# A longer lag between a head's q and k loads and its scores, and the younger of two heads stepped first, in the attention of a streaming Conformer layer

## The chip, the cores and the metric

The kernel runs on one core of a Trainium2 chip. The metric is the device time of one execution in microseconds; the figure for the kernel before is the median of three runs. The profile is that of one further execution, and its own time is given beside its span below.

## The reference

One inference step of a one-layer streaming encoder, in float32, on a prompt of 2048 frames and a sample of 64 frames that has a cache of 256 keys and values. Cut to what matters:

```
h = rms_norm(x, g1) * (1 + sc1) + sh1
z = h @ w_in                         # GLU pair | q | k | v | two gates
u = glu_a * sigmoid(glu_b)           # -> causal depthwise conv, 31 taps
conv_out = silu(layer_norm(conv(u))) @ w_conv_out
q, k = rms_norm per head
s = (q @ k.T) / 8 + rel_bias[clip(q_pos - k_pos)]     # own chunk of 64 and the 8 before it
attn_out = (softmax(s) @ v) @ w_attn_out
x = x + gt1 * ((sig(g_conv) * conv_out + sig(g_attn) * attn_out) @ w_o)
x = x + gt2 * ((silu(gate) * up) @ w_ffn_out)         # gate, up from a normed x
```

There are 8 heads of 64. The outputs are both streams, the last 30 conv rows, and the last or new k and v rows.

## The kernel before, in words

**Two parts.** Part one makes everything up to the attention output and the conv output, which go to DRAM (`o_d`, `c_d`, `g_d`). Part two reads them back, merges them, and runs the output projection and the FFN. Every float32 product is made of three fp32r products of a high and a low part (`mm3`). Each Meter wrapper (L102 is its line, which is why nearly every instruction of the profile has that line) passes an instruction on and adds a planned duration to the load of its engine.

**Part one** runs over four blocks of 512 prompt frames (the first with the 64 sample frames beside them). `ORDER` gives the stages of a block: q projection, conv column group 0, k projection, group 1, v projection, groups 2 and 3, then 16 gate column groups. Through the whole of it TensorE's instructions run in the order in which the program writes them (`manual_schedule`, L1625); the order on the other engines, and that of the DMAs on SP's queue, is laid out by the framework.

**Lanes.** The matmuls of projections, conv groups and gates are the main line. Everything else is written as generators that sit in lanes: norms of the next block, q/k row work, attention (`attn`), conv norm, conv taps. After every 500 ns of planned TensorE time `Stream.tick` gives each lane a turn (`Lane.pump`, L141). A generator yields the planned TensorE time (`stream.load["pe"]`) from which it may be stepped again, or a condition. The lane takes the first of its `wide` oldest generators that is ready. For `attn` that is two wide, one step in 600 ns of plan at most, and none while the plan has VectorE over 3000 ns or ScalarE over 4000 ns ahead (`ATTN`). In block 3 the lane takes up to two steps a tick, without spacing. None of these times is a wait on the chip: they only fix where in TensorE's list a matmul stands. The waits on the chip are semaphores.

**Attention of a block.** After its v projection, `heads` (L1643) adds one generator per head: 8 prompt heads a block, and in block 0 also 8 heads of the sample (`"s"`), alternating with the prompt's; 40 in all, listed in `order`. `attend(i)` (L1495):

1. waits until head i - 1 is scored; `fetch(i)` (L1482) issues q, k (`load_qk`, L1418 and L1419: four DMAs on SP) and the bias band (`load_bias`, L1462: two more), unless the head before did it, and sets `loaded[i]`, the planned time from which scores may be given out.
2. yields `loaded[i]`, then for each of four tiles of 128 queries: four matmuls into `sc` (two PSUM banks, one buffer), VectorE's bias add with running maximum (`softmax_max`), ScalarE's exponential; between tiles it yields until VectorE is planned to be done.
3. after its last tile calls `fetch(i + 1)`. From block 1 on q2, kk and bias have one buffer each, so these loads can't start before the last scores are done.
4. scales, then, once head i - 1 is finished, five rounds of transposes (`ptp`), splits into `ph` and `pl` on ScalarE and VectorE, and products with v into `po`; at the end the output goes to `o_d`.

In block 0 the small q and k tiles of prompt head and sample head have separate places in the same buffers, so q and k of the next but one head are loaded early (`fetch_qk(i + 2)`).

At the end of part one `attn.drain()` (L1686) steps whatever is left, without regard to planned times. Part two's matmuls follow.

The lines that the change and the prediction touch:

```
DMA_LAG = 4000.0                                     # L50
attn = Lane(ATTN, ATTN_NS, wide=2)                   # L1608
entry = next((e for e in self.gens[: self.wide] if self.ready(e, stream)), None)
loaded[i] = stream.load["pe"] + DMA_LAG              # L1488
yield loaded[i]                                      # L1503
```

The planned duration of a matmul of n columns (n of 256 or more) is n / 2.4 ns. `DMA_LAG` also serves weights and other loads.

Of the kernel before, what the change touches and what calls it, by code (L numbers as in the profile page):

```python
# [39 lines left out]
ATTN = {"dve": 3000, "act": 4000}  # L40
ATTN_NS = 600.0
# [6 lines left out]
ON_ACT = (0, "s", 1, 2, 3)  # L48
ON_POOL = ()
DMA_LAG = 4000.0  # L50
OUT_LAG = 4000.0
CACHE_LAG = 16000.0
HEADS_NS = 2000.0
# [31 lines left out]
class Meter:  # L85


    def __init__(self, engine, name, stream):
        self.engine, self.name, self.stream = engine, name, stream
# [18 lines left out]
class Lane:  # L108

    def __init__(self, room, spacing=0.0, wide=1, burst=1):
        self.gens, self.room, self.spacing, self.wide, self.burst = [], room, spacing, wide, burst
        self.last = -1e9

# [25 lines left out]
    def pump(self, stream):  # L141
        for _ in range(self.burst):
            now = stream.load["pe"]
            if now - self.last < self.spacing or stream.full(self.room):
                return
            entry = next((e for e in self.gens[: self.wide] if self.ready(e, stream)), None)
            if entry is None:
                return
            self.last = now
            self.step(entry)  # L150
# [113 lines left out]
class Weights:  # L264
# [107 lines left out]
    def load(self, kind, sure=True):  # L372
# [8 lines left out]
        self.room[tag] -= 1  # L381
        self.landed[i] = self.stream.load["pe"] + DMA_LAG
        if self.items[i][0] == "fi":
# [178 lines left out]
def up_operands(f):  # L562

    ops = (["s2", "s3", "s1"] if f else ["s3", "s2", "s1"]) + ["a22"] + ["a12"] * (f >= EARLY) + ["a11"] * (EARLY <= f + 1 < NF) + ["s4"]
    return [(f + (op == "a11"), op) for op in ops]
# [50 lines left out]
def streaming_layer(ctx: ExitStack, tc: tile.TileContext, I, O):  # L618
    nc = tc.nc
    stream = Stream()  # L620
    pe, dve, act, gps = (
        Meter(e, n, stream) for e, n in ((nc.tensor, "pe"), (nc.vector, "dve"), (nc.scalar, "act"), (nc.gpsimd, "pool"))
    )
# [10 lines left out]
    def rows(prompt, sample, t, n):  # L634
        return prompt[t - SMP : t - SMP + n] if t >= SMP else sample[t : t + n]
# [824 lines left out]
    def load_bias(h):  # L1460
        for r in (0, HD):
            nc.sync.dma_start(  # L1462
                bias[r : r + HD, HD - r : 640 - r],
                bass.AP(tensor=rb_d.tensor, offset=rb_d.offset + 768 * h + HD, ap=[[1, HD], [1, 576]]),
            )
        return bias

    order, loaded, now = [], {}, {"scored": -1, "finished": -1, "bias": None}
# [8 lines left out]
    def fetch_qk(i):  # L1477
        if i < len(order) and ("qk", i) not in now:
            x, h = order[i]
            now["qk", i] = load_qk(x, h, *spans(x))  # L1480

    def fetch(i):  # L1482
        if i < len(order) and i not in loaded:
            x, h = order[i]
            fetch_qk(i)
            if now["bias"] is None or now["bias"][0] != h:
                now["bias"] = h, load_bias(h)
            loaded[i] = stream.load["pe"] + DMA_LAG  # L1488

    def fetch_v(i):  # L1490
        if i < len(order) and ("v", i) not in now:
# [3 lines left out]
    def attend(i):  # L1495
        x, h = order[i]
        q0, nq, k0, nk = spans(x)
        yield lambda: now["scored"] == i - 1
        fetch(i)
        fetch_v(i)  # L1500
        if not i:
# [4 lines left out]
        for t in range(0, nq, P):  # L1506
            n = min(P, nq - t)
            if x not in (0, "s"):
                ps = ps_a.tile([P, 2, 512], F32, tag="s", name="sc")
                for j in range(2):  # L1510
                    for d in range(2):
                        pe.matmul(ps[:, j, :320], q2[:, d, t : t + P], kk[:, t + 320 * j : t + 320 * j + 320], start=d == 0, stop=d == 1)
                w, src, bs = 640, ps[:, :, :320], bias[:, ::-1]
            else:
                w = nk if x == "s" else t + P

                if "banks" not in now:
                    sc = ps_a.tile([P, 2, 512], F32, tag="s", name="sc")
                    now["banks"] = [sc[:, 0:1], sc[:, 1:2]]
                ps = now["banks"].pop(0)  # L1520
                now["banks"].append(ps)
                for d in range(2):
                    pe.matmul(ps[:n, 0, :w], q2[:, d, t : t + n], kk[:, :w], start=d == 0, stop=d == 1)
                src, bs = ps[:n, 0:1, :w], bias[:n, 64:384][:, ::-1] if x == "s" else bias[:, :w][:, ::-1]
            pr, sm, free, ready = softmax_max(src, n, w, bs)
            tiles.append((pr, sm, n, w))
            if t + P < nq:
                yield free + PE_LAG, SCORE_ROOM
            else:
                fetch(i + 1)  # L1530
                if (x, order[min(i + 2, len(order) - 1)][0]) in ((0, 0), ("s", "s")):
                    fetch_qk(i + 2)
                now["scored"] = i
            if t:
                softmax_scale(*tiles[-2], x in ON_ACT)
# [69 lines left out]


    norm_lane, work = Lane({}, wide=NORM_W), Lane({}, wide=5)
    attn = Lane(ATTN, ATTN_NS, wide=2)  # L1608
    conv, tail = Lane({"dve": CONV_ROOM}, burst=4), Lane({})
    stream.lanes = [norm_lane, work, attn, tail, conv]  # L1610

# [268 lines left out]
    for s, (lo, hi) in enumerate(CBLOCKS):  # L1880
# [120 lines left out]
        class Operands:  # L2001


            def __init__(self, f0):
                self.ops = [(e, op) for f in (f0, f0 + 1) for e, op in up_operands(f)]
                self.at = 0
# [154 lines left out]
        def pieces():  # L2161
            return [(i, t, n, j) for i, (t, n) in enumerate(tiles) for j in range(2)]

        def scale():
# [4 lines left out]
            ends["gt"] = gt  # L2169
            yield stream.load["pe"] + DMA_LAG  # L2170
            for k, (i, t, n, j) in enumerate(pieces()):
# [21 lines left out]
        def load_ends():  # L2193
# [3 lines left out]
            for k, (i, t, n, j) in enumerate(pieces()):  # L2197
                nc.sync.dma_start(ends["x1"][k // 3][:n, k % 3], x1_d[t : t + n, 512 * j : 512 * j + 512])
            ends["landed"] = stream.load["pe"] + 2 * DMA_LAG

        def add_last(ws):

            for k, (i, t, n, j) in enumerate(pieces()):
# [14 lines left out]
                else:  # L2218
                    stream.at(stream.when("dve") + OUT_LAG, lambda out=out, dst=dst: nc.sync.dma_start(out, dst))
            for _ in ws:  # L2220
# [4 lines left out]
        def add_left(left):  # L2225

            for dst, x1, out in left:
                gps.tensor_tensor(dst, dst, x1, ALU.add)
                stream.at(stream.when("pool") + OUT_LAG, lambda out=out, dst=dst: nc.sync.dma_start(out, dst))
                yield stream.when("pool"), {"pool": 500}  # L2230

        def add_down(fs, ws):

            last = fs[-1] == NF - 1
            for i, (t, n) in enumerate(tiles):
# [15 lines left out]
                for j, ps in enumerate(pss):  # L2251
# [7 lines left out]
                    else:  # L2259
                        dve.tensor_tensor(ps, ps, dst, ALU.add)  # L2260
                        dst = dst[:n]
                        if t < SMP:
# [3 lines left out]
                        stream.at(  # L2266
                            stream.when("dve") + OUT_LAG,
                            lambda t=t, n=n, f=f, dst=dst: nc.sync.dma_start(rows(y_p, y_s, t, n)[:, f], dst),
# [89 lines left out]
```

## Time and profile before

| | us |
|---|---|
| median of three runs | 3014.24 (3009.83 to 3023.16) |
| profiled execution, its own time | 3015.03 |
| its span in the profile | 3013.2 |
| TensorE busy | 2908.0 |
| mean granted TensorE clock | 0.989 of full |

"A <- B" in a row reads "A waited for B" for waits, and "out <- in" for an instruction. In a timeline row the first number is the start from the beginning of the span, the second the duration, both in us; x4 means four instructions merged, and the bracket holds the idle time of the engine just before and what ended it. A wait for several semaphores is put down to the one that came last by the profile. In a row of waits the numbers are the total in us, the count, and the longest. Part one ends at about 1243 us of the span. `sc` are scores, `ptp` the transposed probabilities, `po` the products with v, `ps` the projections, gates and everything else on the main line; kk and q are a head's k and q.

### The profile page before, as it was taken

How to read it: one execution, taken by the hardware profiler on the slowest of the kernel's cores; microseconds unless marked ns; L12 is line 12 of the kernel's file. 1: busy time of each engine (PE TensorE's matmuls, PEld its weight loads, DVE VectorE, ACT ScalarE, POOL GpSimd, SP SyncE). 2: the span in 40 equal slices, each digit the busy share in tenths (PEclk: the TensorE clock that was granted, in tenths of full speed). 3: DMA queues.
4: the chain of work that ended last, by engine and by line, in shares of the span. 5: the costliest groups of instructions: out<-in, count | busy, mean ns of one | idle time of the engine just before them, and what ended most of it. 6: DMA issues, size and time to landing. Idle time of an engine off the chain costs nothing.

```text
span 3013.2 us, 44846 instructions
## 1 busy us (share of the span) xinstructions
PE 2908.0 (97%) x16193; PEld 2600.1 (86%) x16193; DVE 2049.2 (68%) x3648; ACT 1364.6 (45%) x2453; POOL 1160.9 (39%) x753
## 2 busy tenths in 40 slices
PE   8989998899999988999999999999999999999999
PEld 5889777787788777888999999999999998999998
DVE  5887687567856876568777755676666656566666
ACT  3345633562365245555344425544444344444442
POOL 1101310111011101354466533256666841566667
PEclk9999999999999999999999999999999999999999
DMA  9988889768886778787444696433423875333333
GB/s 315 317 283 296 289 280 305 246 217 274 295 282 206 245 235 251 254 277 247 137 141 150 213 294 207 153 95 113 125 89 121 291 259 182 99 94 112 120 99 129
DMA packets 467067, 628.04 MB, mean 208 GB/s; under 512 B 36196, under 2 KB 314584, under 8 KB 466845
## 3 DMA queue, kind: packets, MB, share of 16 engines
q1 hardware_dynamic: 452944, 606.11, 62.0%
q10 hardware_dynamic: 13901, 19.08, 1.8%
q8 instruction: 127, 2.08, 0.3%
q14 instruction: 95, 0.78, 0.1%
HBM read 476.53 MB, written 148.54 MB: 207 GB/s over the span
## 4 chain that ended last, share of the span: by engine, by line
PE 47%; DVE 2%; ACT 1%; issue 1%; DMA 0%; POOL 0%; ACTq 0%; DVEq 0%
PE ps L102 28%; PE pd L102 14%; PE pw L102 4%; DVE wlo L102 1%; ACT whi L102 1%; DVE ps L102 0%; DMA cin<-o_d 0%; ACT xn L102 0%; DVE acc L102 0%; DMA tg<-g_d 0%; DVE sums L102 0%; PE pt L102 0%; ACT t L102 0%; DVE hid L102 0%; ACT hid L102 0%
## 5 line engine op out<-in xcount | busy, mean ns | idle before, releaser
L102 PE MATMUL ps<-t,whi 128*128 128x384 f32 (+1 forms) x2112 | 501.9, 322 | 2.8 <-ACT u L102 0.8
L102 POOL TENSOR_TENSOR wlo<-wst,whi 128x1024 fp32r<-128x1024 f32 (+1 forms) x159 | 362.9, 2294 | 248.7 <-ACT whi L102 229.1
L102 ACT ACTIVATE whi<-wst 128x1024 fp32r<-128x1024 f32 (+1 forms) x265 | 258.3, 979 | 311.5 <-PE ps L102 125.4
L102 PE MATMUL ps<-b,whi 128*128 128x384 f32 (+1 forms) x1584 | 380.6, 325 | 5.1 <-DVE v L102 2.1
L102 PEld LDWEIGHTS ps<-t,whi 128*128 128x128 f32 x2112 | 367.8, 188 | 10.1 <-ACT u L102 3.3
L102 DVE SCALAR_TENSOR_TENSOR y<-u,wd,y 128x512 f32<-128x512 f32 (+1 forms) x480 | 371.1, 774 | 7.3
L102 PE MATMUL ps<-hh,whi 128*128 128x512 f32 (+2 forms) x992 | 367.2, 370 | 0.0
L102 DVE TENSOR_TENSOR acc<-acc,pd 128x512 f32<-128x512 f32 x482 | 322.2, 685 | 47.9 <-PE pd L102 45.4
L102 PE MATMUL ps<-hh,wlo 128*128 128x512 f32 (+2 forms) x992 | 348.0, 351 | 0.0
L102 PE MATMUL ps<-hl,whi 128*128 128x512 f32 (+2 forms) x992 | 347.8, 351 | 0.0
L102 PE MATMUL ps<-t,wlo 128*128 128x384 f32 (+1 forms) x1056 | 338.4, 321 | 0.0
L102 PE MATMUL pd<-whi,hid 128*128 128x512 f32 x912 | 297.5, 391 | 0.5 <-DVE acc L102 0.3
L102 PEld LDWEIGHTS ps<-b,whi 128*128 128x128 f32 x1584 | 276.9, 188 | 13.3 <-DVE v L102 3.2
L102 ACT ACTIVATE pr<-pr,sm 128x640 f32<-128x640 f32 (+3 forms) x272 | 200.8, 748 | 168.3 <-DVE sm L102 164.8
L102 POOL TENSOR_TENSOR r<-t,mhalf 128x1 f32<-128x1 f32 (+2 forms) x68 | 83.7, 1232 | 466.1 <-DVE t L102 448.6
L102 PE MATMUL ps<-b,wlo 128*128 128x384 f32 (+1 forms) x792 | 256.1, 323 | 0.0
L102 PEld LDWEIGHTS ps<-hh,wlo 128*128 128x128 f32 x992 | 189.2, 191 | 23.1
L102 PEld LDWEIGHTS ps<-hh,whi 128*128 128x128 f32 x992 | 190.4, 192 | 18.2 <-issue 2.5
L102 DVE TENSOR_TENSOR wlo<-wst,whi 128x1024 fp32r<-128x1024 f32 (+1 forms) x106 | 136.4, 1291 | 98.2 <-ACT whi L102 96.8
L102 PEld LDWEIGHTS ps<-hl,whi 128*128 128x128 f32 x992 | 190.2, 192 | 14.9 <-issue 1.9
L102 PEld LDWEIGHTS pd<-whi,hid 128*128 128x128 f32 x912 | 171.2, 188 | 36.8 <-DVE acc L102 1.3
L102 PEld LDWEIGHTS ps<-t,wlo 128*128 128x128 f32 x1056 | 198.1, 188 | 0.8
(233 smaller groups left out, 6307.3 us busy)
## 6 DMA issues: line engine op xcount, KB each, us to landing
whi<-w_din_h SPq DMA_DIRECT2D x72, 512.0 KB, 6.8
wlo<-w_din_l SPq DMA_DIRECT2D x72, 512.0 KB, 7.4
wst<-sum_d SPq DMA_DIRECT2D x131, 256.0 KB, 2.8
wfo<-in_w_ffn_out SPq DMA_DIRECT2D x64, 512.0 KB, 3.9
wmod<-in_w_ada SPq DMA_DIRECT2D x46, 512.0 KB, 9.2
sum_d<-ws SPq DMA_DIRECT2D x88, 256.0 KB, 2.3
wst<-in_w_ffn_in SPq DMA_DIRECT2D x85, 256.0 KB, 3.2
wst<-in_w_in SPq DMA_DIRECT2D x40, 512.0 KB, 6.9
```

The source lines that it names most:

```text
L102: self.last = f(*args, **kw)
```

## The change

Two constants are added and one condition, and a lane gets a flag.

- The planned time from which a head's scores may be given out, counted from the point where its loads are written, is 9000 ns instead of 4000. For the first head of block 0, of block 2 and of block 3 it is 14000. (The first head of block 1 comes after a sample head, so the condition leaves it at 9000, as it does sample heads.)
- In the attention lane, of the two oldest generators the younger is asked first whether it is ready; before, it was the older. The other lanes are unchanged, and so are `push` and `drain`.

No instruction is added or removed; the order of TensorE's instructions in part one changes, and with it what the framework makes of the other engines' order.

```
+QK_LAG = 9000.0
+FIRST_LAG = 14000.0
...
-    def __init__(self, room, spacing=0.0, wide=1, burst=1):
+    def __init__(self, room, spacing=0.0, wide=1, burst=1, young=False):
+        self.young = young
...
-            entry = next((e for e in self.gens[: self.wide] if self.ready(e, stream)), None)
+            order = self.gens[: self.wide]
+            entry = next((e for e in (order[::-1] if self.young else order) if self.ready(e, stream)), None)
...
-            loaded[i] = stream.load["pe"] + DMA_LAG
+            first = x != "s" and (not i or order[i - 1][0] not in (x, "s"))
+            loaded[i] = stream.load["pe"] + (FIRST_LAG if first else QK_LAG)
...
-    attn = Lane(ATTN, ATTN_NS, wide=2)
+    attn = Lane(ATTN, ATTN_NS, wide=2, young=True)
```

## The prediction

> **What bounds the kernel now.** I read the page first: the busy row of each engine, then the windows by stage, then TensorE's waits, then the single instructions around one of them.
>
> ```profile
> span 3013.2 us, 44846 instructions
> PE 2908.0 (97%) x16193; PEld 2600.1 (86%) x16193; DVE 2049.2 (68%) x3648; ACT 1364.6 (45%) x2453; POOL 1160.9 (39%) x753
> ```
> ```profile
> 0.00:160.00 160.00, 143.63 (x849) 112.68 (x850) 116.17 (x209) 58.31 (x87) 26.70 (x31) 1.00 0.92 311
> 160.00:455.00 295.00, 278.34 (x1770) 248.89 (x1769) 233.22 (x485) 145.53 (x330) 47.51 (x46) 0.98 0.87 290
> 455.00:760.00 305.00, 282.49 (x1546) 235.52 (x1545) 207.33 (x396) 130.54 (x237) 31.54 (x30) 0.97 0.81 261
> 760.00:1045.00 285.00, 272.37 (x1448) 229.12 (x1447) 203.54 (x389) 131.16 (x239) 30.54 (x30) 0.97 0.78 251
> 1045.00:1245.00 200.00, 180.13 (x918) 151.73 (x917) 128.84 (x243) 108.70 (x188) 25.09 (x17) 0.97 0.77 241
> 1245.00:3013.20 1768.20, 1751.03 (x9673) 1622.12 (x9671) 1160.07 (x1928) 790.36 (x1372) 999.50 (x601) 1.00 0.51 166
> ```
>
> The columns are busy time of PE, PEld, DVE, ACT and POOL, then TensorE's granted clock, DMA share and GB/s. TensorE sets the end. Its order is given in part one and that part is all the diff touches, so only its idle time and its slow clock can be won. The four attention stages (160 to 1245) hold 16.7 + 22.5 + 12.6 + 19.9 = 71.7 us of idle and a clock of 0.97 to 0.98; part two, 1768 us long, idles 17. What ends the idle time:
>
> ```profile
> PE sc L102 <- DMA kk<-k_d: 50.3, 13, 8.9
> PE sc L102 <- DVE hl L102: 3.5, 1, 3.5
> PE sc L102 <- DVE y L102: 3.0, 1, 3.0
> PE sc L102 <- DVE sm L102: 2.2, 3, 1.5
> ```
>
> Thirteen waits of score matmuls for k loads make 50.3 us. The rows of 3.5 and 3.0 are a head's first score too, with its loads just under way; I count them to the loads. That gives **56.8 us over 15 heads** of 40. One of them, with the loads ahead of it:
>
> ```profile
> 505.51 0.74 PE L102 MATMUL sc<-kk,q 128*128 128x320 f32 x4
> 513.97 0.82 PE L102 MATMUL sc<-kk,q 128*128 128x320 f32 x4 [2.93 <-DMA kk<-k_d]
> 529.99 0.74 PE L102 MATMUL sc<-kk,q 128*128 128x320 f32 x4
> ```
> ```profile
> 506.29 0.60 SPq L1418 DMA_DIRECT2D q<-q_d  x1
> ...
> 508.24 0.60 SPq L1419 DMA_DIRECT2D kk<-k_d  x1
> 508.94 1.20 SPq L1462 DMA_DIRECT2D bias<-rb_d  x2
> ```
>
> The last score of the old head runs at 505.51. Its single q2 and kk buffers come free and SP issues the four loads; the last lands at 513.97, 8.5 us after 505.51. TensorE reached the next score at 513.97 - 2.93 = 511.04, 5.5 us after 505.51: the 4 us lag of the plan plus a step. Then the younger head's second score comes only at 529.99, because the older head is served first.
>
> A stall costs again after it, in clock:
>
> ```profile
> 172.25:182.25 10.00, 10.00 (x58) 10.00 (x59) 7.48 (x15) 4.32 (x9) 0.66 (x3) 0.75 0.82 254
> ...
> 513.97:523.97 10.00, 10.00 (x47) 8.37 (x48) 8.91 (x16) 4.52 (x8) 0.00 (x0) 0.83 0.91 344
> ...
> 602.24:612.24 10.00, 10.00 (x55) 8.46 (x56) 4.09 (x8) 5.75 (x12) 0.00 (x0) 1.00 0.75 291
> ...
> 1145.80:1155.80 10.00, 10.00 (x51) 8.81 (x52) 6.27 (x13) 5.94 (x12) 0.00 (x0) 0.83 0.43 149
> ```
> ```profile
> 573.99 0.63 PE L102 MATMUL ps<-hl,whi 128*128 128x512 f32 x1
> 574.42 0.63 PE L102 MATMUL ps<-hh,wlo 128*128 128x512 f32 x1
> ...
> 577.48 0.39 PE L102 MATMUL ps<-hl,whi 128*128 128x512 f32 x1
> 577.71 0.40 PE L102 MATMUL ps<-hh,wlo 128*128 128x512 f32 x1
> ```
>
> The first fence is the 10 us after a restart (4 of 15 such stretches). A clock of 0.83 there is 3.4 us at half speed. Over the 15 stretches (1 - clock) x 20 us sums to 41 us; four stretches show none. At half speed matmuls start 0.43 us apart, against 0.23, so a half-speed microsecond loses 0.47: **19 us**.
>
> The clock is where a page bears on this. The Trainium skill, TensorE: Matmul & The Clock Gate, What's actually happening, says that the gate falls to half after about 3.4 us of idleness and rises after 3.4 us of work. The trace agrees in the half speed and the length but not in the threshold: the wait of 2.93 us was followed by 0.83. By the page only the six waits of over 3.4 us would pay, about 11 us instead of 19, and the forecast below would be 8 us higher; I go by the trace.
>
> **The change, part by part.** *The lag (9 instead of 4 us).* It adds no instruction and takes none away. The loads keep their place behind the last score of the head before; the score matmuls move back behind some 5 us more of projection matmuls, past whatever weight loads SP issues meanwhile. The plan counts 0.213 us for a 512-column matmul (512 / 2.4) that takes 0.23, so 5 us of plan is 5.4 on the chip, and TensorE arrives about 5.5 + 5.4 = 10.9 us after the last score. In the steady part 11 heads stalled; the landing is the first score's start minus the last score before it. The slowest and the last of them:
>
> ```profile
> 562.11 0.85 PE L102 MATMUL sc<-kk,q 128*128 128x320 f32 x4
> 572.36 1.41 PE L102 MATMUL sc<-kk,q 128*128 128x320 f32 x4 [4.62 <-DMA kk<-k_d]
> ...
> 1183.52 0.74 PE L102 MATMUL sc<-kk,q 128*128 128x320 f32 x4
> 1191.75 0.82 PE L102 MATMUL sc<-kk,q 128*128 128x320 f32 x4 [2.70 <-DMA kk<-k_d]
> ```
>
> They landed after 10.3 and 8.2 us, and the others between: all are covered. VectorE's maximum and ScalarE's exponential move with the scores; POOL has no part. What hides the 5.4 us is the projection and gate work; where that is gone, the full wait would show (third rival).
>
> Two heads aren't covered by it:
>
> ```profile
> 453.54 0.32 SPq L1060 DMA_DIRECT2D v_d<-vst  x1
> 454.45 0.45 SPq L1419 DMA_DIRECT2D kk<-k_d  x1
> ```
> ```profile
> 467.14 1.41 PE L102 MATMUL sc<-kk,q 128*128 128x320 f32 x4 [7.73 <-DMA kk<-k_d]
> ...
> 1058.94 0.74 PE L102 MATMUL sc<-kk,q 128*128 128x320 f32 x4
> 1075.42 1.41 PE L102 MATMUL sc<-kk,q 128*128 128x320 f32 x4 [3.05 <-DMA kk<-k_d]
> ```
>
> The first head of block 1 gets 9 us and not 14 (the head before it is "s"); its loads sit on SP behind a v store. It arrives at 459.4 + 5.4 and the load lands at 467.1: 2.3 us stay, with 1.6 of clock, so 4. The second head of block 3 has its load 16.5 us after the last score (1058.94 to 1075.42), against an arrival at 10.9: 5.6 us idle and 2 of clock, or nothing if the crowd of loads has passed by then; I take 4, the middle.
>
> *FIRST_LAG (14 us)* works on heads 0, 24 and 32 of the list. Head 0 waited longest:
>
> ```profile
> 172.25 0.66 PE L102 MATMUL sc<-kk,q 128*128 128x128 f32 x2 [8.93 <-DMA kk<-k_d]
> ```
>
> It was reached at 163.3; 10 us of plan more put it at 174, after the load. The firsts of blocks 2 and 3 showed no wait for k; they just start later.
>
> *The younger head first.* With the older first, scoring and the value products take turns: in block 1 a head needs 28 us (505.51 to 562.11 is two heads). Now scores go as soon as they are ready. The chain per head becomes 10.9 us of lag plus three gaps of 2 to 3.3 us, some 17 to 21 us, and the softmax and value products of the older head, which end some 24 us after its last score (505.51 to 529.99, with 2.9 of stall), lie beside it instead of ahead of it. In block 0 q and k are fetched a head further ahead, so the lag buys nothing there after head 0; the scores come later under other work, and I cost that at nothing, since block 1's projections cover it and its heads queue behind. The price is that half of the heads, which used to be reached late and so never waited, are now reached at 10.9 us too. No row shows their landings. From below it is nothing, if they land as the 11 did; from above, at the 2.9 us of the row at 513.97 with 1.6 of clock for each of some 12 such heads, 54 us. I take 6 us, because the observed landings all lie under 10.9. A score of the younger head also waits for VectorE to clear the one score bank, amid the older head's splits. Today's waits of that kind are the 2.2 us above; from below nothing, as the plan holds the next score until VectorE is due; I add 2, the same again.
>
> **The sum.** 56.8 + 19 = 76 us can go; 4 + 4 + 6 + 2 = 16 stay or come back. 60 us off the profiled execution's own 3015.0 (its span is 3013.2) is **2955 us**. The median of the runs, 3014.24, is 0.8 lower, which I neglect. With nothing coming back it is 2939; with 40 us coming back, 2979.
>
> **The rivals.**
>
> *Late loads take half of it.* TensorE does the same work in 61 us less, so the loads of stages 160 to 1245 (mean DMA share 0.81 by the windows) press into 1024 us: 0.86. For it speaks the landing of 16.5 us above. Against it: in 0 to 160 DMA ran at 0.92 and TensorE, once started, hardly waited for weights. Another 2 us for 15 heads makes 46 us that come back instead of 16: **2985**, and 2997 with 1.6 of clock on half of them.
>
> A page speaks for that one: the Trainium skill, DMA: Bandwidth & Descriptors, Issuing engines are not separate DMA queues, says all issuing engines share the same 16 DMA engines and interleave. No run here separates that.
>
> *The change doesn't do what it says.* The lag is a moment in the plan, not a wait. If the stalls only went elsewhere (a bias load that VectorE needs comes 2.7 us after the first q load, so it could be the next to be late), 76 would go and as much come back: **3015**. Against it: VectorE's groups name a bias load as releaser for 10.2 us in all, three times.
>
> ```profile
> L102 DVE CUSTOM_DVE_ANT_0 pr<-sc,bias 128x640 f32<-128x640 f32 (+5 forms) x136 | 98.0, 720 | 79.3 <-PE sc L102 66.5 <-DMA bias<-rb_d 10.2 <-PE ps L102 0.9
> ```
>
> *The end of part one pays (slower).* Block 3's attention is the last thing; what is left after the gates is drained with no other work between.
>
> ```profile
> 1231.21 0.74 PE L102 MATMUL sc<-kk,q 128*128 128x320 f32 x4
> ...
> 1234.54 0.27 PE L102 MATMUL pt<-ident,gates_c 128*32 128x128 f32 x1
> ```
>
> Today the last score comes 3.3 us before the last gate work. From 1058.94 to 1231.21 seven heads took 172 us; 16 of the stage's 19.9 idle are these waits, and some 6 are clock, so a head is 21.5 us of work. Starting 10 us later, eight heads still fit if one takes no more than (172 - 22 + 3.3 - 10) / 7 = 20.5 us; I expect 17 to 21, so the margin is thin. A head in the drain would idle about 20 us (8.5 for its loads, four rounds of score and maximum at some 2 us, the softmax), with clock 22. One head left costs 22 and leaves 2977; from the fourth on the gain is gone. That needs 40 us a head, about double; with four left **3043**. The Trainium skill, Perfetto Trace Analysis, Optimization Strategy, says that consistent bubbles can mean too few buffers; by that rule a lag only shifts what a second kk buffer would remove, as in this rival.
>
> **How the numbers follow.** Forecast (2936 to 2979) 0.66; better than 2936, 0.04; half gain (2979 to 2999) 0.16; no change (2999 to 3029) 0.08; slower 0.06. The range leaves out the last two and most of the best case: 2936 to 2997. A measurement of this kernel can tell 0.5%, 15 us, from no change: faster 0.86, same 0.08, slower 0.06.
>
> **What would show it.** Right: waits of score matmuls for k loads fall from 50 us to under 15; the granted clock of the four stages rises to 0.99; last scores of neighbouring heads in block 1 lie 17 to 21 us apart instead of 28, with value products between one head's scores. Wrong: waits for kk or for bias stay above 30 us; more than one head's scores follow the last gate; a wait for weights takes their place; or part two changes its 1768 us.

## The result, and the profile after

The changed kernel takes 2963.27 us (median of four runs, 2962.06 to 2966.65) against 3013.33 of the kernel before beside it: a ratio of **0.983, interval 0.981 to 0.986**. The forecast was 2955, the range 2936 to 2997. The profiled execution took 2963.89, with a span of 2962.2. The helper's line is now L104, and `load_qk` is L1422 and L1423.

The page's span and busy row, then the windows by the same stages as before (busy time of PE, PEld, DVE, ACT, POOL; clock; DMA share; GB/s):

```profile
span 2962.2 us, 44854 instructions
PE 2895.4 (98%) x16193; PEld 2589.7 (87%) x16193; DVE 2048.5 (69%) x3648; ACT 1364.2 (46%) x2453; POOL 1161.0 (39%) x753
```
```profile
0.00:160.00 160.00, 141.75 (x835) 110.69 (x835) 114.28 (x206) 57.00 (x86) 26.52 (x31) 1.00 0.91 307
160.00:455.00 295.00, 282.86 (x1786) 252.79 (x1785) 236.29 (x482) 146.19 (x328) 46.50 (x46) 0.98 0.89 297
455.00:760.00 305.00, 296.69 (x1656) 245.86 (x1655) 223.77 (x424) 133.94 (x247) 31.69 (x31) 0.99 0.87 281
760.00:1045.00 285.00, 282.58 (x1497) 238.66 (x1497) 217.12 (x416) 137.74 (x251) 31.59 (x30) 0.99 0.83 266
1045.00:1245.00 200.00, 190.67 (x1036) 165.12 (x1035) 122.74 (x245) 116.44 (x194) 42.25 (x22) 0.97 0.84 259
1245.00:2962.20 1717.20, 1700.85 (x9391) 1576.54 (x9390) 1134.26 (x1878) 772.92 (x1350) 982.49 (x593) 1.00 0.50 162
```

Span less busy is TensorE's idle time: 3013.2 - 2908.0 = 105.2 before, 2962.2 - 2895.4 = 66.8 now. So of 51.0 us, **38.4 are idle time that went and 12.6 are busy time**, with the same 16193 matmuls, about what the clock gives (worked out below). The first three attention stages idle 12.1 + 8.3 + 2.4 instead of 16.7 + 22.5 + 12.6. The last two rows aren't like for like, since part two now starts inside the fifth. Part two's first matmul starts at 1192.28, in the kernel before at 1243.36, and what follows lasts 1769.9 us, then 1769.8: all of the gain lies in part one.

TensorE's waits in part one (total, count, longest):

```profile
PE sc L104 <- DVE sm L104: 13.2, 10, 5.7
PE sc L104 <- DMA kk<-k_d: 6.0, 3, 4.7
```

The k loads, 56.8 us over 15 heads with the two rows counted to them, are down to 6.0 over three. But `sm`, VectorE's maximum that clears the score bank, is up from 2.2 to 13.2. Less 50.8 and more 11.0 make 39.8 us of idle time gone; all other waits together took 1.4 of it back, which leaves the 38.4.

Scores of block 1, from the timeline, with one product with v between them:

```profile
480.34 0.74 PE L104 MATMUL sc<-kk,q 128*128 128x320 f32 x4
496.01 1.40 PE L104 MATMUL sc<-kk,q 128*128 128x320 f32 x4 [4.69 <-DMA kk<-k_d]
...
508.98 0.79 PE L104 MATMUL sc<-kk,q 128*128 128x320 f32 x4
520.06 0.83 PE L104 MATMUL sc<-kk,q 128*128 128x320 f32 x4
...
522.12 0.39 PE L104 MATMUL po<-ph,vv 128*128 128x512 f32 x1
...
523.71 0.74 PE L104 MATMUL sc<-kk,q 128*128 128x320 f32 x4
...
530.52 0.81 PE L104 MATMUL sc<-kk,q 128*128 128x320 f32 x4
541.55 0.74 PE L104 MATMUL sc<-kk,q 128*128 128x320 f32 x4
```

From the last score of one head (508.98, 530.52) to the first of the next are 11.1 and 11.0 us, with no wait in a bracket, and the older head's products lie between the younger's scores. Both parts of the change do what they say. The first head of the fence is the exception: reached at 11.0 us (496.01 - 4.69 - 480.34) as the others, its load landed only at 15.7.

Two things are new. One is the end of part one. From the last gate matmul to part two's first, as windows of the kernel before and of this one:

```profile
1234.81:1243.36 8.55, 5.61 (x37) 4.33 (x35) 4.24 (x7) 5.28 (x10) 2.79 (x2) 1.00 0.48 156
```
```profile
1173.87:1192.28 18.41, 12.31 (x57) 9.85 (x55) 8.11 (x18) 10.08 (x19) 2.37 (x1) 0.72 0.22 75
```
```profile
1173.60 0.27 PE L104 MATMUL pt<-ident,gates_c 128*32 128x128 f32 x1
...
1176.97 0.79 PE L104 MATMUL sc<-kk,q 128*128 128x320 f32 x4
1178.69 1.43 PE L104 MATMUL sc<-kk,q 128*128 128x320 f32 x4 [0.93 <-DVE sm L104]
...
1182.72 0.47 PE L104 MATMUL ptp<-ident,pr 128*128 128x128 f32 x1 [2.17 <-ACT pr L104]
```

The last two scores now follow the last gate. Idle time there is 6.1 us instead of 2.9, and 7.1 of the 12.3 busy us fall into 10.2 us at a clock of 0.51 (the last window in the part on the clock), so about 3.2 + 7.1 x 0.47 = 6.5 us are lost. The other new thing is the longest of the `sm` waits, in block 0, with TensorE, SP and VectorE around it:

```profile
387.40 0.33 PE L104 MATMUL sc<-kk,q 128*128 128x128 f32 x2
...
396.08 0.80 PE L104 MATMUL sc<-kk,q 128*128 128x256 f32 x2 [5.70 <-DVE sm L104]
```
```profile
382.61 0.36 SPq L1053 DMA_DIRECT2D q_d<-part_l  x1
383.76 1.74 SPq L1429 DMA_DIRECT2D vv<-v_d  x1
...
386.12 1.19 SPq L1466 DMA_DIRECT2D bias<-rb_d  x2
```
```profile
395.75 0.27 DVE L104 CUSTOM_DVE_ANT_0 pr<-sc,bias 128x128 f32<-128x128 f32 x1
```

The head's bias loads stand on SP behind q stores and v loads and are issued 1.3 us before the score at 387.40. VectorE takes that score up only at 395.75, 8 us after its end; in these it does other work and waits once, 1.53 us, for POOL. The experiments ask which of the two it is.

### The profile page after: what moved, and what is told of

It reads as the page before. It is cut to its first block, busy times and chain, and to the rows that moved or that the text cites. A ratio compares the mean times of both kernels' runs of the same rounds, so it can differ in the third digit from the quotient of the medians.

```text
span 2962.2 us, 44854 instructions
## 1 busy us (share of the span) xinstructions
PE 2895.4 (98%) x16193; PEld 2589.7 (87%) x16193; DVE 2048.5 (69%) x3648; ACT 1364.2 (46%) x2453; POOL 1161.0 (39%) x753
## 4 chain that ended last, share of the span: by engine, by line
PE 47%; DVE 2%; ACT 1%; DMA 1%; issue 1%; POOL 0%; SPq 0%; ACTq 0%; DVEq 0%
PE ps L104 28%; PE pd L104 14%; PE pw L104 5%; DVE wlo L104 1%; ACT whi L104 0%; DVE ps L104 0%; DMA cin<-o_d 0%; DMA wst<-in_w_conv_out 0%; DMA x<-x_d 0%; ACT xn L104 0%; DMA wfo<-in_w_ffn_out 0%; DMA tg<-g_d 0%; DVE sums L104 0%; PE pt L104 0%; ACT t L104 0%
## 5 line engine op out<-in xcount | busy, mean ns | idle before, releaser
L104 PE MATMUL ps<-t,whi 128*128 128x384 f32 (+1 forms) x2112 | 501.8, 322 | 2.9 <-DVE u L104 0.9
L104 POOL TENSOR_TENSOR wlo<-wst,whi 128x1024 fp32r<-128x1024 f32 (+1 forms) x159 | 363.4, 2297 | 241.8 <-ACT whi L104 231.1
L104 ACT ACTIVATE whi<-wst 128x1024 fp32r<-128x1024 f32 (+1 forms) x265 | 258.2, 979 | 314.1 <-PE ps L104 131.5
L104 PE MATMUL ps<-b,whi 128*128 128x384 f32 (+1 forms) x1584 | 380.5, 325 | 5.8 <-DVE v L104 2.1
L104 PEld LDWEIGHTS ps<-t,whi 128*128 128x128 f32 x2112 | 367.7, 188 | 10.2 <-ACT u L104 3.3
L104 DVE SCALAR_TENSOR_TENSOR y<-u,wd,y 128x512 f32<-128x512 f32 (+1 forms) x480 | 369.9, 773 | 7.6
L104 PE MATMUL ps<-hh,whi 128*128 128x512 f32 (+2 forms) x992 | 362.9, 366 | 0.1
L104 DVE TENSOR_TENSOR acc<-acc,pd 128x512 f32<-128x512 f32 x482 | 322.2, 685 | 48.8 <-PE pd L104 46.1
L104 PE MATMUL ps<-hh,wlo 128*128 128x512 f32 (+2 forms) x992 | 345.2, 348 | 0.0
L104 PE MATMUL ps<-hl,whi 128*128 128x512 f32 (+2 forms) x992 | 345.0, 348 | 0.0
L104 PE MATMUL ps<-t,wlo 128*128 128x384 f32 (+1 forms) x1056 | 338.2, 321 | 0.0
L104 PE MATMUL pd<-whi,hid 128*128 128x512 f32 x912 | 297.1, 390 | 0.3 <-DVE hid L104 0.3
L104 PEld LDWEIGHTS ps<-b,whi 128*128 128x128 f32 x1584 | 276.7, 188 | 14.1 <-ACT early L104 3.4
L104 ACT ACTIVATE pr<-pr,sm 128x640 f32<-128x640 f32 (+2 forms) x272 | 201.3, 749 | 148.7 <-DVE sm L104 143.9
L104 PE MATMUL ps<-b,wlo 128*128 128x384 f32 (+1 forms) x792 | 256.0, 323 | 0.0
L104 POOL TENSOR_TENSOR r<-t,mhalf 128x1 f32<-128x1 f32 (+2 forms) x68 | 81.8, 1210 | 423.3 <-DVE t L104 411.2
L104 PEld LDWEIGHTS ps<-hh,wlo 128*128 128x128 f32 x992 | 187.0, 189 | 22.7
L104 DVE TENSOR_TENSOR wlo<-wst,whi 128x1024 fp32r<-128x1024 f32 (+1 forms) x106 | 134.7, 1274 | 103.0 <-ACT whi L104 101.8
L104 PEld LDWEIGHTS ps<-hh,whi 128*128 128x128 f32 x992 | 187.8, 189 | 18.2 <-issue 2.9
L104 PEld LDWEIGHTS pd<-whi,hid 128*128 128x128 f32 x912 | 171.1, 188 | 36.0 <-ACT hid L104 0.7
L104 PEld LDWEIGHTS ps<-hl,whi 128*128 128x128 f32 x992 | 188.0, 190 | 14.7 <-issue 1.7
L104 PEld LDWEIGHTS ps<-t,wlo 128*128 128x128 f32 x1056 | 198.0, 188 | 0.8
```

The lines of the kernel that those rows point to most:

```text
L104: self.last = f(*args, **kw)
```

## The experiments

Each edit is against the changed kernel, each ratio against the kernel before on the same chip. Theory A is the prediction's account: the lag takes the waits, younger-first gives the longer chain of each head room beside the older head.

**The lag alone.**

```
-    attn = Lane(ATTN, ATTN_NS, wide=2, young=True)
+    attn = Lane(ATTN, ATTN_NS, wide=2)
```

> The longer lags, with the older head asked first as before. Theory A (the lag removes the waits for k, and younger-first is what keeps the attention short enough to end with part one): waits of scores for kk under 12 us in all, but a head of block 1 takes 28 to 31 us from last score to last score instead of 22, and in block 3 one or two heads are left after the last gate at some 20 us each: 2970 to 2995 us. Rival B (the lag does it all, the order of the two heads is indifferent): 2955 to 2967 us, with the end of part one as in the changed kernel.

Measured: 2981.01 us, 0.988 (0.986 to 0.989). No first score waits for k, and the last gate runs at 1170.44, 3 us earlier than with the whole change. But part two starts at 1211.42, 19.1 us later, as the profiled span is longer (2981.6 against 2962.2). The window from the last gate to part two:

```profile
1170.71:1211.42 40.71, 27.71 (x124) 21.51 (x122) 18.59 (x41) 22.99 (x42) 2.34 (x1) 0.71 0.31 89
```

Two whole heads are scored behind the last gate: 13.0 us idle and a clock of 0.71. What younger-first buys on top of the lag is the end of part one, not the waits for k. The waits for `sm` come with the lag too: in part one they are, here and then with younger first alone (the next run):

```profile
PE sc L104 <- DVE sm L104: 18.2, 18, 3.8
```
```profile
PE sc L104 <- DVE sm L104: 1.8, 2, 1.1
```

Of the 18.2 us, 6.9 lie behind the last gate. The prediction's slower rival does act here, at a smaller price: against the kernel before, 10.1 us more idle time and 5 to 11 us of clock, some 15 to 21 us for two heads, where it put 22 on one. (A clock of 0.71 over 40.71 us is 23.6 us at half speed; at 0.47 that is 11, or 5 if all 13 idle us lie within it.)

**Younger first alone.**

```
-QK_LAG = 9000.0
-FIRST_LAG = 14000.0
+QK_LAG = 4000.0
+FIRST_LAG = 4000.0
```

> The younger head first, with the old lag of 4 us for all heads. Theory A: now every head from block 1 on is reached about 5.5 us after the last score, where loads land after 8.2 to 10.3, so some 24 to 30 waits of about 3 us each and a half-speed stretch after half of them: waits for kk 75 to 100 us, time 3020 to 3060 us, slower than the kernel before. Rival C (it is the order of the heads that helps, since scores no longer stand between two value products): waits for kk at most as before, 2960 to 3005 us.

Measured: 3034.05 us, 1.006 (1.004 to 1.008): **slower than before**. Waits of part one, and first scores of heads:

```profile
PE sc L104 <- DMA kk<-k_d: 62.9, 10, 15.4
```
```profile
171.81 0.66 PE L104 MATMUL sc<-kk,q 128*128 128x128 f32 x2 [7.17 <-DMA kk<-k_d]
477.73 1.41 PE L104 MATMUL sc<-kk,q 128*128 128x320 f32 x4 [10.06 <-DMA kk<-k_d]
...
1137.73 0.82 PE L104 MATMUL sc<-kk,q 128*128 128x320 f32 x4 [2.90 <-DMA kk<-k_d]
```

A was right on the sign and partly on the cause. In block 3 six heads, each reached 5.2 to 5.9 us after the last score, waited for k (2.7 to 7.6 us), and a seventh, reached at 7.3, idled 2.3 us under another name; in the kernel before five of the seven had waited. In blocks 1 and 2 only the first head of block 1 and the second heads of both waited (10.06, 7.04, 15.43); the rest were reached at 10.7 to 19 us for another reason, which the runs don't settle. So the waits are 62.9 us and not the 75 to 100 of A. Part two starts 11.0 us later than in the kernel before (1254.39 against 1243.36); the other 6.4 us by which this profile is longer lie in part two, where the edit changes nothing. The two halves don't add: medians move by -35 for the lag alone and +18 for the order alone, but by -50 together.

**How long the lag must be.**

```
-QK_LAG = 9000.0
+QK_LAG = 13000.0
```

> 13 us of plan for each head instead of 9 (first heads 14), younger first. Theory A: waits for kk under 3 us, a head of block 3 takes 24 us instead of 20, and one to two heads are left after the last gate: 2970 to 3000 us, slower than the changed kernel's 2963. Rival B (a longer lag can only cover more loads): 2950 to 2962 us.

Measured: 2976.46 us, 0.986 (0.985 to 0.988). No wait for k of 1 us is left, and two heads follow the last gate (a tail of 41.7 us at a clock of 0.71): the price of a lag beyond the landing is paid at the end.

```
-QK_LAG = 9000.0
+QK_LAG = 7000.0
```

> 7 us of plan instead of 9 (first heads 14), younger first. Theory A: a head is reached about 5.5 + 3.2 = 8.7 us after the last score; of loads that land after 8.2 to 10.3, half show a wait of up to 1.6 us: waits for kk 8 to 20 us, few of them long enough for half speed, and the chain of block 3 is 2 us a head shorter, so nothing is left after the last gate: 2955 to 2972. Rival F (what counts is any longer lag, the landing time is not the threshold): waits for kk as with 9 us, 6 us or less, and a time under 2955.

Measured: 2970.34 us, 0.985 (0.983 to 0.987). In block 3 six of the seven later heads are reached at 8.3 to 9.2 us, the other at 10.9; waits for k in part one are 7.6 us over four heads and two other first scores wait 2.7 and 2.2. The tail is 4.3 us long, without a score in it. Not told apart from 9 us: a few us more of waits against a shorter tail.

**The longer lag of first heads.** First at 9 us like the rest, then kept for head 0 alone:

```
-FIRST_LAG = 14000.0
+FIRST_LAG = 9000.0
```

> 9 us of plan for the first heads too, instead of 14. Theory A: head 0 is reached some 5 us earlier and waits 3 to 4 us for its k load again, with 2 us of clock; block 3's attention starts 5 us earlier, so less of it is left after the last gate (idle and half speed there cost some 8 us in the changed kernel): within 5 us of the changed kernel, 2958 to 2968. Rival D (the loads of a block's first head are what the 14 us are for in every block): first heads of blocks 2 and 3 wait 3 us or more each as well: 2970 to 2978.

```
-            first = x != "s" and (not i or order[i - 1][0] not in (x, "s"))
+            first = not i
```

> 14 us of plan for head 0 alone; the first heads of blocks 2 and 3 get 9 as all others. Theory A (the tail after the last gate is what the changed kernel pays for starting block 3 later): no wait of head 0, block 3's last score before the last gate again, part two's first matmul within 10 us of the last gate instead of 18.7: 2952 to 2962 us. Rival D (blocks 2 and 3 need the 14 us): waits for kk at their first heads, 2962 to 2975.

Measured: 2970.87 us, 0.984 (0.983 to 0.986), and 2962.51 us, 0.982 (0.980 to 0.984). Neither is told apart from the changed kernel. In the first, head 0 waits 1.68 us for k and 1.74 for `sm`. In the second the tail is 8.5 us again, at full clock, yet the time stays: it idles 2960.7 - 2893.4 = 67.3 us, as much as the 66.8, since other waits took what the tail gave back (2.2 us of a first score behind a weight load among them). So the 14 us of blocks 2 and 3 are worth nothing that shows.

**Are the new `sm` waits VectorE's backlog, or the bias load?** First every further score of a head 1.5 us later in the plan, to give VectorE time:

```
-                yield free + PE_LAG, SCORE_ROOM
+                yield free + PE_LAG + 1500.0, SCORE_ROOM
```

> In the changed kernel each further score of a head is given out 1.5 us of plan later. Theory A: the 13 us of waits of scores for VectorE (sm) come from the plan having VectorE done too early, so they fall under 4 us; but each head of block 3 takes some 4 us more, and one to two heads are left after the last gate, some 10 to 25 us more there: 2960 to 2985. Rival E (these waits are loads of the bias band, which a later score doesn't cure): sm waits stay above 9 us.

Measured: 2988.92 us, 0.991 (0.989 to 0.993). `sm` waits are 12.0 us over seven: six in the tail, where two heads are now left, and one of 5.18 in block 0, at another head than before (221.05), at which VectorE itself idled 4.28 us for the bias load. The small ones ahead of the tail went, as a backlog would; a large one stayed. The later scores cost more at the end (a tail of 39.9 us) than they brought.

Then the bias band loaded once for all heads, which leaves out every later head's own bias (on top of the 14 us for head 0 alone):

```
-            if now["bias"] is None or now["bias"][0] != h:
+            if now["bias"] is None:
...
-            first = x != "s" and (not i or order[i - 1][0] not in (x, "s"))
+            first = not i
```

> The kernel with 14 us for head 0 alone, and the bias band loaded once, for head 0, and used for every head: it leaves out the bias loads of 7 heads in each block, 62 DMAs. Theory H (the waits of scores for VectorE in block 0 are bias loads that come late, behind a v load that holds SP's queue): the waits for sm in 160 to 455 fall from 10 to 12 us to under 3, the half speed after them goes, 2940 to 2953 us. Rival I (VectorE is simply behind with other work there): these waits stay at 7 us or more, 2953 to 2965.

Measured: 2953.82 us, 0.979 (0.977 to 0.981). In 160 to 455, this kernel beside the one that only has its lag rule, 14 us for head 0 alone:

```profile
PE sc L104 <- DVE sm L104: 4.8, 4, 1.6
```
```profile
PE sc L104 <- DVE sm L104: 11.6, 6, 5.7
```

The 4.8 us lie between what the two theories on record named, under 3 and 7 or more, and both were half right: the waits of 3.1 and 5.7 us hang on the bias load and go with it, those of up to 1.6 us stay.

Last, the whole bias, but issued on ScalarE's queue (with the lag rule of the next run):

```
-            nc.sync.dma_start(
+            nc.scalar.dma_start(
...
-            first = x != "s" and (not i or order[i - 1][0] not in (x, "s"))
+            first = not i or i == 2 * NH + 1
```

> 14 us of plan for head 0 and for the second head of block 1, and every bias band loaded by ScalarE's queue instead of SP's. Theory H (in SP's queue the bias stands behind q stores and a v load that wait, which costs block 0 its waits for VectorE): these waits in 160 to 455 fall from 10.4 us to 5 or less as with one bias band, and no bias load holds up an exponential for long: 2943 to 2955 us, the fastest of all. Rival K (on ScalarE's queue the load waits there for the last maximum and holds up exponentials and splits behind it): waits for pr or ph on TensorE rise by 5 us or more, 2955 to 2970.

Measured: 2959.02 us, 0.980 (0.978 to 0.982). The waits of 160 to 455:

```profile
PE sc L104 <- DVE sm L104: 4.8, 4, 1.6
```

The same row to the digit as without the loads; with the bias on SP's queue and the same lag rule (the next run) it was 10.4. So at a lag of 9 us it is **the bias load's place on SP's queue** that makes the long waits. It isn't the only cure: in the run with 13 us, where the bias stayed on SP, the waits of the same stretch were

```profile
PE sc L104 <- DVE sm L104: 1.7, 2, 1.1
```

so the moment of the scores counts as well. TensorE's waits for the exponential and its splits didn't grow. But first scores of blocks 1 to 3 now waited again (k loads 5.0 us over five heads, 4.9 and 2.5 under other names), and no gain over the next run is left.

**The second head of block 1**, the last long wait for k, gets 14 us, as head 0 does; the first heads of blocks 2 and 3 have 9:

```
-            first = x != "s" and (not i or order[i - 1][0] not in (x, "s"))
+            first = not i or i == 2 * NH + 1
```

> 14 us of plan for head 0 and for the second head of block 1, 9 for all others. Theory A (that one head's load lands 15.5 us after the last score, behind block 1's other loads): its wait of 4.7 to 5.0 us and some 2 of clock go, nothing else changes: 2950 to 2960 us, some 6 below the kernel with 14 us for head 0 alone. Rival J (the wait comes from the loads' late issue in SP's queue, and moves with the scores): the wait stays above 3 us, 2958 to 2966.

Measured: 2957.42 us, 0.979 (0.978 to 0.981), the lowest time of all but the kernel with one bias band. The last score of the first head and the first of the second in its timeline:

```profile
479.71 0.75 PE L104 MATMUL sc<-kk,q 128*128 128x320 f32 x4
...
495.94 0.75 PE L104 MATMUL sc<-kk,q 128*128 128x320 f32 x4
```

The head is reached at 16.2 us and waits for nothing; the longest wait of a first score is 0.96. The changed kernel, run once more beside it, unedited:

> The changed kernel again, on the chip of the two others: 2960 to 2967 us by the first measurement; says whether the differences of a few us between versions can be told from one chip to the next.

Measured: 2962.71 us, 0.982 (0.980 to 0.983), with `sm` 13.8 and k 7.3 us. The 5 us between the two are as large as the wait that went, but their intervals overlap, and the two differ in the first heads of blocks 2 and 3 as well.

**The longer lag with the older head first, but short in block 3**, so that its tail is spared:

```
-            first = x != "s" and (not i or order[i - 1][0] not in (x, "s"))
-            loaded[i] = stream.load["pe"] + (FIRST_LAG if first else QK_LAG)
+            first = not i
+            loaded[i] = stream.load["pe"] + (FIRST_LAG if first else DMA_LAG if x == 3 else QK_LAG)
...
-    attn = Lane(ATTN, ATTN_NS, wide=2, young=True)
+    attn = Lane(ATTN, ATTN_NS, wide=2)
```

> The longer lag without younger-first, and in block 3 the old 4 us (head 0 has 14). Theory A: the loss of the lag alone, 2981 against 2963, is all in what is left after the last gate of block 3. With the old lag there block 3 has its old waits (16 us and some 6 of clock) and the old end, while blocks 0 to 2 keep the gain: 2960 to 2975. Rival G (the older-first order costs in blocks 1 and 2 as well): 2976 to 2990.

Measured: 2986.69 us, 0.990 (0.988 to 0.992). The number fell where the rival on record put it, but not by its mechanism: blocks 1 and 2 (455 to 760, 760 to 1045) idle 6.0 and 6.3 us, 12.2 together, against 10.7 of the changed kernel. The tail is 8.5 us, and block 3 waits for k again:

```profile
PE sc L104 <- DMA kk<-k_d: 12.6, 4, 3.5
```

A's figure was too low by a sum wrongly made (2963 + 22 for block 3's waits and clock - 7 for the tail is 2978, not 2960 to 2975) and by block 0, which idles 18.0 us from 160 to 455 (295.00 - 277.05) against 12.1. So with the older first, block 3 can either wait for its loads or drain; only with the younger first it does neither in full.

A second buffer for kk and q was not tried: by the kernel's tiles it needs 8 KB more in each partition of the on-chip memory.

## Why the prediction was right, and what was off

**Right: the waits and their cause.** Of the 21 heads of blocks 1 to 3 that follow another of their block, TensorE reaches 15 at 10.2 to 11.1 us, worked out as 10.9, and six at 12.3 to 15.0; all but three find their loads landed; 15 waits are three. **The newly reached heads** were put at 6 us between 0 and 54; one of them waited, 0.50 (the wait of 0.83 is at the fifth head of block 3, which had waited 3.74 before). The nearest rows, the eleven observed landings, were the right guide.

**Right in kind, one head off: what the lag doesn't cover.** The 8 us were for the first head of block 1 and the second of block 3. Neither waited. Block 0's heads now end later, and the first head of block 1 starts its scores at 467.62. The uncovered head is the second of block 1, as SP's part of the timeline shows:

```profile
480.42 0.37 SPq L248 DMA_DIRECT2D wmod<-in_w_ada  x1
481.69 0.60 SPq L1422 DMA_DIRECT2D q<-q_d  x1
482.94 0.47 SPq L1423 DMA_DIRECT2D kk<-k_d  x1
484.22 0.60 SPq L1422 DMA_DIRECT2D q<-q_d  x1
485.58 0.45 SPq L1423 DMA_DIRECT2D kk<-k_d  x1
```

After the last score at 480.34 the last of its four loads is issued only at 485.58 (in the example of the prediction it took 2.7 us), behind weight loads. Cost 4.7 us and clock; 8 was put in for two heads. The price was about right, the place wrong: where a load meets a crowd depends on the new order and wasn't to be read off the old trace.

**Mis-sized: "I add 2, the same again", the waits for `sm`.** It was 11.0. This is the largest miss, and the term stood in the wrong place: 9.8 of the 13.2 us lie in block 0 (160 to 455), whose later scores the prediction costed at nothing, and by the two runs with half of the change they come with the lag (18.2 us) and not with the younger head first (1.8). The prediction held the bias load to be next late only as a rival in which all the gain goes, and weighed it by VectorE's idle time behind bias. That group's row hardly moved (10.2 before; the last column here):

```profile
L104 DVE CUSTOM_DVE_ANT_0 pr<-sc,bias 128x640 f32<-128x640 f32 (+5 forms) x136 | 97.8, 719 | 33.1 <-PE sc L104 22.2 <-DMA bias<-rb_d 9.9
```

For most of the 5.70 us that TensorE waits VectorE isn't idle; it does other work that stands ahead in its order. The runs show that at this lag the load's place on SP decides it. How far VectorE is held at run time and how far the framework put its instruction later because of the load is left open.

**About right: the clock.** 19 us were to go, and some 4 of what was to stay or come back were clock too; TensorE's busy time fell by 12.6. Whole-run clock is 0.989 before and 0.994 now, (1 - clock) x 2 x span: 66 and 36 us of half speed, and 30 x 0.47 is 14. The four stages have 0.98, 0.99, 0.99 and 0.97 where 0.99 was the sign named for all. Most of what is left goes with the new waits. Three 10 us windows of the changed kernel:

```profile
311.00:321.00 10.00, 10.00 (x52) 9.15 (x51) 7.86 (x18) 6.87 (x18) 5.95 (x4) 0.83 0.98 344
393.00:403.20 10.20, 7.12 (x23) 6.11 (x24) 8.68 (x22) 3.27 (x10) 0.21 (x1) 0.51 0.89 306
...
1178.00:1188.20 10.20, 7.09 (x26) 5.76 (x27) 4.58 (x11) 5.67 (x10) 0.00 (x0) 0.51 0.17 67
```

The second begins inside the 5.70 us wait, the third is the tail, and the first follows a wait of 2.41 us. That is again below the 3.4 us of the Trainium skill, TensorE: Matmul & The Clock Gate, What's actually happening, as the prediction had it from one of 2.93.

**The end of part one: "the margin is thin".** Heads of block 1 were to be 17 to 21 us apart and are 22.5 ((637.79 - 480.34) / 7 between their last scores), since from head to head there are 11.9 us on average, not 10.9, and the gaps between a head's scores average 3.5 and reach 5.4 us, not 3.3. In block 3 they are 20.0 ((1178.69 - 1038.51) / 7), within the 20.5 that were to be enough. But from the first head's last score to the last gate there are 135.1 us (1173.60 - 1038.51), where the prediction had 143.3 (172 - 22 + 3.3 - 10), so seven heads (140.2) end 5.1 us behind the gate. It cost about 6.5 us that the sum didn't hold. The rival's 22 us a head measured 8 to 10 with the lag alone: there the second of the two heads' first score ran 12.2 us after the last score before it (1192.28 - 1180.11) with no wait for its load, as other products stood between. (By its own 22 us a head the gain of 60 would have been gone with the third head, not the fourth.)

**Rivals.** No wait for weights came in place of those for k. A general lateness of loads at a higher DMA share (0.83 to 0.89 in the three stages, 0.78 to 0.87 before) isn't seen at heads reached at 10 us. With the one buffer the waits for k fell from 56.8 to 6.0 us. The Trainium skill, Perfetto Trace Analysis, Optimization Strategy, says that consistent bubbles can mean too few buffers; here most of them went without a second one.

In sum: 60 was forecast and 51 came. Against the forecast stand 9 us more of `sm` and some 6.5 of the tail; for it 5.5 of newly reached heads that didn't wait and 1 to 2 of the uncovered one. So the forecast came as near as it did in part because terms that were missed on both sides cancel.

## What to carry to other kernels

Where an engine runs a fixed order, place a consumer behind the landing that the trace shows under load, and then look at two places: what the same queue delivers next (here the bias), and what the longer chain leaves behind the last independent work. A lag and a change of order needn't add: here the medians moved by -35 us for the one, +18 for the other and -50 for both, so test them singly and jointly before one is given up. A wait of a non-bottleneck engine's group says little about how late that engine serves the bottleneck: follow one instance across all three.

## What was not expected of the hardware

The first 50 us, in which attention has no part, show a granted clock of 1.00, 0.93 or 0.86, by kernel. The windows of the lag alone, and of the changed kernel in its second profile (the run beside the second head's):

```profile
0.00:50.00 50.00, 34.25 (x210) 21.30 (x210) 25.80 (x67) 17.61 (x25) 5.17 (x14) 0.86 0.92 295
```
```profile
0.00:50.00 50.00, 36.01 (x220) 22.55 (x224) 26.67 (x68) 17.73 (x25) 4.79 (x14) 1.00 0.94 305
```

That column can't be trusted at the very start. The same two matmuls of the changed kernel, in its first profile and in its second:

```profile
26.83 0.39 PE L104 MATMUL ps<-wlo,hh 128*64 128x512 f32 x1
27.05 0.39 PE L104 MATMUL ps<-whi,hl 128*64 128x512 f32 x1
```
```profile
26.65 0.63 PE L104 MATMUL ps<-wlo,hh 128*64 128x512 f32 x1
27.08 0.63 PE L104 MATMUL ps<-whi,hl 128*64 128x512 f32 x1
```

Starts 0.43 us apart are half speed, as in the prediction's rows, though the window says 1.00 in both. So the second profile starts with more slow matmuls than the first, of one and the same kernel. The Trainium skill, TensorE: Matmul & The Clock Gate, What's actually happening, says that the activity window runs free, so one kernel can start with differing numbers of slow matmuls; these two profiles agree. What it costs is small: the first `pa<-sel,R` after the start of `ps` runs at 29.35 and 30.19 in these two and at 30.94 with the lag alone, whose window says 0.86. Differences of a few us between the runs can't be put down to the clock that the first 50 us show.
